# The first head's k and q projections are queued on TensorE behind the last pair's index scores of the two longest blocks

## The chip, the core and the metric

The kernel runs on one core of a Trainium2 chip. The metric is the device time of one execution in microseconds (us). The engines are TensorE (PE in the rows), VectorE (DVE), ScalarE (ACT), GpSimd (POOL) and SyncE (SP), which here only issues transfers. Each engine runs its own list of instructions in the order of the built program, so an instruction that waits holds up all that stand behind it on that engine.

## The reference, cut to what matters

One residual block over 1024 tokens of width 1024. Its mixer has two groups of heads; all their inputs come from one projection of the normed x.

```python
proj = h @ w_in
q_a, c_kv, q_idx, k_idx, w_idx, q_b, k_b, v_b, a_b, b_b, z_b = jnp.split(proj, split_points, axis=-1)
# sparse attention, per block of 128 queries
rel = jax.nn.relu(jnp.einsum('bqhd,bsd->bqhs', qi_b, k_idx))
score = jnp.einsum('bqhs,bqh->bqs', rel, wi_b)
_, idx = lax.top_k(score, topk)              # topk = 256; the chosen keys are attended to
# gated DeltaNet, 4 heads: conv and silu of q, k, v, then a recurrence over chunks of 64
t_inv = lax.linalg.triangular_solve(eye + lower, ...)
```

After the mixer come the output projection and a squared-ReLU MLP, with a norm before and behind each.

## The kernel before, in words

Products are taken in three matmuls with operands split into a high and a low part (`mm3`, L192, the matmuls are L199 to L201). A projection of 128 columns is 2 halves x 8 slices x 3 = 48 matmuls of 512 columns into one of two PSUM buffers called `two` (`project_slowly`, L333).

The stage in question, up to about 430 us, runs these generators, of which `Flow.run` (L114) picks the next by a model of time and their rank; a scheduler then sets the final order on each engine.

- `projections` (L952) goes through the plan kw, qi0 to qi3, then kb and qb of heads 0 to 3, vb0 to vb3, z0 to z3, c, qa0 to qa3. kw and qi feed the index scores; the 20 behind qi3 and kb0 (qb0 to qa3) and kb0 itself feed the rest. After kb, qb and vb a `conv` follows: one pass on ACT (L587), three on DVE (L589), a SiLU on ACT (L592). After each qb, `delta_head` (L675) makes transposes (L684), norms (L688) and Gram products (L705, L706) of that head.
- `scoring` (L460): for each pair of index heads p = 0 to 3, each block b = 7 down to 2 and each piece of its keys (320 to 512 columns) and each of the two heads, two matmuls (L471, L472) into a bank `tr` or `ch` (two of each), a ReLU on ACT in place (L478), and a multiply and add into `score` on DVE (L479). That is 80 pieces.
- `bisect` (L494) waits for "scored", the end of all scores. It finds the 256th largest score of every row bit by bit: 32 steps, each with three passes on ACT (L521) and three on DVE (L528), and a small update (L531 to L533; of the first step L536 to L538), which the next step needs. Then come the ties and the mask for six blocks (L549 to L578), on DVE.
- `base_blocks` (L711), after head 3: 31 dependent pairs of DVE operations (L725, L726) invert the diagonal blocks, a copy (L727) ends them, SP stores the result (L728) and loads it back (`diagonals`, L740).
- `levels` (L765) and `chain` (L857), which need that: POOL builds `ui` and `te` (L783), then matmuls L797, L806, L810, L822, L830, L838 alternate with small copies on ACT and DVE (L798, L807, L812, L823, L831, L839), and L870 is the first product of the recurrence.
- `post_c` (L421) ends with two DVE passes over `c_row` (L436, L437). The next stage begins with the transposes of `c_row` on TensorE (L1098) and, on SP, with loads of queries (L1057) and of w_uk and w_uv (L1089), which ACT splits (L1092) for the keys' products. L1288 loads a gain into the place of `c_row` once the transposes have read it; it is used much later.

In the kernel before, nothing but rank and the model of time sets kb0, qb0 and the following projections against the scores.

Of the kernel before, what the change touches and what calls it, by code (L numbers as in the profile page):

```python
# [18 lines left out]
P = 128  # L19
# [120 lines left out]
def block_kernel(ctx: ExitStack, tc: tile.TileContext, x, w_in, c_norm, w_uk, w_uv, rel_bias, conv_w, a_log,  # L140
# [4 lines left out]
    V, S, G, PE, SY = nc.vector, nc.scalar, nc.gpsimd, nc.tensor, nc.sync  # L145
# [18 lines left out]
    const, _ = pl.open("const")  # L164
    ps_t, _ = pl.open("ps_t", bufs=2, space=PSUM)
    ps_c, _ = pl.open("ps_c", bufs=2, space=PSUM)
    ps_w, ps_w_close = pl.open("ps_w", bufs=2, space=PSUM)
    dram, _ = pl.open("dram", space=DRAM)
# [106 lines left out]
    loaded = {}  # L275
# [12 lines left out]
    ps = psw()  # L288
# [15 lines left out]
    ps = pst()  # L304
# [3 lines left out]
    for half in range(2):  # L308
# [9 lines left out]
        for k in range(NK):  # L318
            ps = pst()
# [13 lines left out]
    def project_slowly(wts, evac, ths=(0, 1), two=False):  # L333
        wh, wl, n = wts
        both = psw() if two else None
        for th in ths:
            sl = slice(th * 512, th * 512 + 512)
            ps = both[:, sl] if two else psa()
            for k in range(NK):
                mm3(ps[:n, :], wh[:, k, :n], wl[:, k, :n], hTH[:, k, sl], hTL[:, k, sl], k == 0, k == NK - 1, True)  # L340
                yield
            evac(ps, th, sl)
        if two:
            loaded["both"] = both
# [26 lines left out]
    QS = pl.t(pi, [P, 8, T], F32R, "QS")  # L371
    KH = pl.t(pi, [P, T], F32R, "KH")
    KL = pl.t(pi, [P, T], F32R, "KL")
# [65 lines left out]
    def bias():  # L439
# [17 lines left out]
        src = bass.AP(tensor=tv_d.tensor, offset=tv_d.offset, ap=[[384, 8], [0, P], [1, 384]])  # L457
        SY.dma_start(tz_d, src)

    def scoring():  # L460

        for p in range(4):
            yield ("qi", p)
            for b in range(NB - 1, 1, -1):
                for s0, w in cuts(P * (b + 1)):
                    dst = score[:, soff[b] + s0:soff[b] + s0 + w]
                    for h in (2 * p, 2 * p + 1):
                        while flow.bank("px", 4) > flow.now:
                            yield flow.bank("px", 4)
                        ps = psx()  # L470
                        PE.matmul(ps[:, :w], QS[:, h, b * P:(b + 1) * P], KH[:, s0:s0 + w], start=True, stop=False)  # L471
                        PE.matmul(ps[:, :w], QS[:, h, b * P:(b + 1) * P], KL[:, s0:s0 + w], start=False, stop=True)  # L472
                        wh = wab[:, b, h:h + 1]
                        t = flow.pe(2 * w / 2260)
                        if h == 0:
                            V.tensor_scalar(dst, ps[:, :w], 0.0, wh, op0=OP.max, op1=OP.mult)
                        else:
                            S.activation(ps[:, :w], ps[:, :w], AF.Relu)  # L478
                            V.scalar_tensor_tensor(dst, ps[:, :w], wh, dst, op0=OP.mult, op1=OP.add)  # L479
                            t = act(t, w / 1200 + 0.18)  # L480
                        flow.took("px", dve(t, w / 960 + 0.16))
                        yield 0.0
        for b in range(NB - 1, 1, -1):
            G.memset(score[0:64, soff[b] + P * b + 64:soff[b] + P * (b + 1)], PAD)
        flow.done("scored", flow.rings["px"][-1])
# [256 lines left out]
    flow = Flow()  # L742
# [209 lines left out]
    def projections():  # L952
        nonlocal dna, dn, dn_close
        for i, (kind, p) in enumerate(plan):
            for j in range(1, 3):
                fetch(i + j)
            evac = None
            if kind == "kw":
                evac = evac_kw
            elif kind == "qi":  # L960
                evac = evac_pair(QS, p, 0.125)
            elif kind in ("kb", "qb", "vb"):
                def evac(*_):
                    pass
            elif kind == "z":
                evac = evac_spill(z_d[:, :, p, :].rearrange("n p t -> p n t"), AF.Silu, 1.0, tmp4())
            elif kind == "c":
                evac = evac_c
            else:
                evac = evac_spill(qa_d[:, p, :].rearrange("p (n t) -> p n t", t=P), AF.Copy, 0.125, tmp4())  # L970
            for _ in project_slowly(loaded[i], evac, two=True):
                flow.pe(0.64)
                yield 0.0
            if kind == "kw":
                post_kw()
                gates()
                bias()
            elif kind == "qi":
                flow.done(("qi", p), dve(act(flow.now, 1.2), 1.4))
            elif kind in ("kb", "qb", "vb"):  # L980
                blk = {"qb": 0, "kb": 4, "vb": 8}[kind] + p
                if kind == "vb":
                    conv(loaded["both"], blk, v_d[:, :, p, :])
                    act(dve(act(flow.now, 1.05), 3.7), 1.1)
                else:
                    act(dve(act(flow.now, 1.05), 3.7), 1.1)
                    if p == 0:
                        for n in range(4 * (kind == "qb"), 4 + 4 * (kind == "qb"), 2):
                            decays(n)
                    if kind == "qb" and p == 0:  # L990
                        yield "scored"
                        pi_close()
                        dna, dna_close = pl.open("dna", side="right")
                    if kind == "kb":
                        kqh = pl.t(dna if p % 2 else kq, [P, NB, 2, P], F32, "kqh")
                    a = 0 if kind == "kb" else 1
                    conv(loaded["both"], blk, q_d[:, :, p, :] if a else None, kqh[:, :, a, :])
                    if kind == "qb":
                        delta_head(p, kqh)
                        dve(act(flow.pe(5.2), 4.0), 9.5)  # L1000
                    if (kind, p) == ("qb", 3):
                        base_blocks()
                        dna_close()
                        kq_close()
                        dn, dn_close = pl.open("dn", side="right")
                        st["dt"] = pl.t(dn, [P, 2, 32, 32], F32, "dt")
                        diagonals()
                        flow.done("base", dve(flow.now + 3.0, 30.0) + 8.0)
            elif kind == "c":
                post_c()  # L1010
        yield "topk"
        flow.done("projections", flow.now)
# [16 lines left out]
    ps_a, _ = pl.open("ps_a", bufs=2, space=PSUM)  # L1029
    ps_s, _ = pl.open("ps_s", bufs=2, space=PSUM)  # L1030
# [377 lines left out]
    hlp, _ = pl.open("hl", bufs=12)  # L1408
# [45 lines left out]
    rawp, _ = pl.open("raw", bufs=2, side="right")  # L1454
    tmpp, _ = pl.open("tmp2", bufs=17, side="right")
# [119 lines left out]
    while ready:  # L1575
# [4 lines left out]
        ps = bank_[{2: 1, 3: 5, 4: 7}.get(j, j)]  # L1580
# [138 lines left out]
    while ready:  # L1719
# [8 lines left out]
        for t in range(4):  # L1728
            ps = bank_[set_][t]
# [9 lines left out]
    fin, _ = pl.open("fin")  # L1739
    rows = []  # L1740
    for f in range(NS):
# [5 lines left out]
        w = []  # L1747
# [21 lines left out]
    for tb in range(NB):  # L1769
        yt = [acc[n][:, tb % 4] for n in (("11", "12"), ("21", "22"))[tb // 4]]  # L1770
        for c in range(2):
            ps = psc() if c else pss()
# [33 lines left out]
```

## Time and profile before

| | |
|---|---|
| median of 3 runs | 1387.98 us (1382.74 to 5743.25) |
| the profiled execution | 1387.9 us |
| its span | 1386.2 us, mean granted TensorE clock 0.965 |
| TensorE / VectorE busy over the span | 93% / 80% |
| first and last score matmul (L471, L472) | 67.8 and 192.3 us |
| first step of the bisection done | 203.3 us |
| transposes of `c_row` (L1098), which open the next stage | 430.63 us |

Times in rows are counted from the span's start. A busy share over the whole span averages over stages with different limits; what the change touches lies between 70 and 440 us and is read from the rows of that stretch. PEclk is the granted clock of TensorE as a share of 2.4 GHz.

### The profile page before, as it was taken

To read this page: it belongs to the slowest core of one execution; us is meant where nothing else is said; L and a number is where in the kernel's file an instruction comes from. 1 tells how busy PE (TensorE), PEld (TensorE's weight loads), DVE (VectorE), ACT (ScalarE), POOL (GpSimd) and SP (SyncE) were. 2 spreads that over 40 slices of the span, in tenths; PEclk is the share of its full clock that TensorE was granted. 3 is DMA by queue.
4 is the path that set the end of the run, shared out by engine and by line. 5 is a ranking of instruction groups with operands and counts; after the bars stand their busy time and mean duration, and the time that the engine had idled before them with its cause. 6 is when DMAs were issued, how large, how long until landed. Compare 5 with 4: busy or idle time off the path is not lost.

```text
span 1386.2 us, 20222 instructions
## 1 busy us (share of the span) xinstructions
PE 1284.0 (93%) x6628; PEld 1110.4 (80%) x6628; DVE 1108.2 (80%) x2552; ACT 735.4 (53%) x1543; POOL 253.7 (18%) x276
## 2 busy tenths in 40 slices
PE   7899999888777999998989899999999899999995
PEld 4578888777666999877878788888887788888885
DVE  5555779999998888987677467888777987888886
ACT  5455457676624777776455456566666333333422
POOL 3112322122233444348020000000000000000023
PEclk8999999999987999999999899999999999999998
DMA  6223224445055332324355916655566975746215
GB/s 195 66 88 106 61 77 122 137 140 134 23 142 155 97 114 81 93 86 162 125 180 185 298 67 213 213 204 196 208 213 239 392 259 203 251 120 206 77 52 176
DMA packets 184146, 213.33 MB, mean 154 GB/s; under 512 B 28161, under 2 KB 123626, under 8 KB 183914
## 3 DMA queue, kind: packets, MB, share of 16 engines
q1 hardware_dynamic: 184042, 212.06, 47.2%
q8 instruction: 52, 0.85, 0.2%
q14 instruction: 52, 0.43, 0.1%
HBM read 138.58 MB, written 75.00 MB: 154 GB/s over the span
## 4 chain that ended last, share of the span: by engine, by line
PE 65%; DVE 19%; DMA 7%; ACT 5%; issue 2%; POOL 0%; SPq 0%; DVEq 0%; ACTq 0%
PE sc L199 4%; PE sc L200 4%; PE sc L201 4%; PE ch L201 4%; PE ch L199 4%; PE ch L200 4%; PE acc L199 4%; PE acc L200 4%; PE acc L201 4%; DVE pre L528 3%; PE two L199 3%; PE two L200 3%; PE two L201 3%; PE tr L199 2%; PE tr L201 2%
## 5 line engine op out<-in xcount | busy, mean ns | idle before, releaser
L199 PE MATMUL two<-hTH,wh 128*128 128x512 f32 (+1 forms) x416 | 164.5, 398 | 23.0 <-ACT tmp L409 10.6
L200 PE MATMUL two<-hTL,wh 128*128 128x512 f32 (+1 forms) x416 | 163.9, 394 | 0.0
L201 PE MATMUL two<-hTH,wl 128*128 128x512 f32 (+1 forms) x416 | 162.0, 391 | 0.0
L1763 POOL TENSOR_TENSOR tmp<-acc,c_row 128x512 f32<-128x512 f32 x16 | 20.7, 1301 | 644.1 <-DVE acc L1776 632.5
L521 ACT ACTIVATE jk<-score,cand 128x1024 bf16<-128x1024 f32 (+2 forms) x96 | 92.4, 964 | 46.8 <-DVE cand L533 36.2
L199 PEld LDWEIGHTS two<-hTH,wh 128*128 128x128 f32 (+1 forms) x416 | 80.6, 194 | 38.9 <-issue 19.7
L200 PEld LDWEIGHTS two<-hTL,wh 128*128 128x128 f32 (+1 forms) x416 | 80.8, 194 | 11.7 <-issue 0.5
L201 PEld LDWEIGHTS two<-hTH,wl 128*128 128x128 f32 (+1 forms) x416 | 80.1, 193 | 12.0 <-issue 0.5
L1426 ACT CAST hl<-raw 128x512 fp32r<-128x512 f32 x81 | 48.6, 614 | 71.4 <-PE acc L200 51.5
L269 POOL TENSOR_TENSOR wl<-stg,wh 128x1024 fp32r<-128x1024 f32 (+1 forms) x26 | 61.1, 2351 | 80.7 <-ACT wh L266 79.3
L1426 ACT CAST hl<-tt 128x512 fp32r<-128x512 f32 x56 | 34.4, 616 | 72.9 <-PE tr L200 44.6
L1426 ACT CAST hl<-tmp 128x512 fp32r<-128x512 f32 x60 | 35.8, 617 | 55.9 <-DVE tmp L1543 30.6
L1427 DVE TENSOR_TENSOR hl<-raw,hl 128x512 fp32r<-128x512 f32 x81 | 55.2, 684 | 4.5 <-ACT hl L1426 3.3
L1187 ACT CAST part<-tr 128x512 fp32r<-128x512 f32 x80 | 42.7, 542 | 27.3 <-PE tr L1185 24.0
L1162 ACT ACTIVATE big<-big,nm 128x256 f32<-128x256 f32 (+6 forms) x64 | 50.4, 789 | 11.3 <-DVE nm L1161 9.4
L1188 DVE TENSOR_TENSOR part<-tr,part 128x512 fp32r<-128x512 f32 x80 | 50.0, 629 | 4.3 <-ACT part L1187 4.0
L1210 PE MATMUL acc<-part,VS 128*128 128x256 f32 x288 | 51.7, 303 | 0.7 <-DVE part L1188 0.7
L268 POOL TENSOR_SCALAR wh<-stg 128x1024 fp32r<-128x1024 f32 x19 | 19.9, 1049 | 174.8 <-PE two L200 160.6
L589 DVE SCALAR_TENSOR_TENSOR tmp<-two,svT,tmp 128x1023 f32<-128x1023 f32 (+2 forms) x36 | 45.9, 1276 | 6.1 <-ACT tmp L587 6.0
L1138 POOL TENSOR_TENSOR mt<-tz,maskb 128x256 f32<-128x256 f32 x56 | 37.6, 681 | 59.3 <-DVE mx L1154 46.2
L199 PE MATMUL acc<-h2H,hl 128*128 128x512 f32 x120 | 46.3, 387 | 1.6 <-ACT tmp L1477 1.6
L1185 PE MATMUL tr<-ident,big 128*128 128x128 f32 x288 | 46.7, 277 | 0.5 <-DVE part L1188 0.4
(507 smaller groups left out, 4121.7 us busy)
## 6 DMA issues: line engine op xcount, KB each, us to landing
hid<-tmp SPq DMA_DIRECT2D x140, 256.0 KB, 2.6
hq<-hid SPq DMA_DIRECT2D x80, 256.0 KB, 5.3
raw<-in_w_mlp_in_dram SPq DMA_DIRECT2D x14, 1024.0 KB, 5.5
tmp<-hid SPq DMA_DIRECT2D x56, 256.0 KB, 5.4
raw<-in_w_mlp_out_dram SPq DMA_DIRECT2D x13, 1024.0 KB, 7.4
stg<-in_w_in_dram SPq DMA_DIRECT2D x25, 512.0 KB, 4.3
x<-in_x_dram SPq DMA_DIRECT2D x8, 512.0 KB, 5.3
la_d<-la SPq DMA_DIRECT2D x8, 512.0 KB
```

Source lines behind the costliest of these rows:

```text
L199: PE.matmul(o, lh, rh, start=start, stop=False, skip_group_check=more)
L200: PE.matmul(o, lh, rl, start=False, stop=False, skip_group_check=more)
L201: PE.matmul(o, ll, rh, start=False, stop=stop, skip_group_check=more)
L269: G.tensor_sub(wl[:, :, :n], f[:, :, :n], wh[:, :, :n].bitcast(F32))
L521: S.activation(junk[:, :n], s_of(b), AF.Sign, bias=cand[:, 3 + i:4 + i].bitcast(F32), scale=-1.0, accum_out=cnt[:, 3 + i:4 + i])
L589: V.scalar_tensor_tensor(acc[:, 3 - j:T], both[:, 0:T - 3 + j], w[j], acc[:, 3 - j:T], op0=OP.mult, op1=OP.add)
L1162: S.activation(pr[:, :n], pr[:, :n], AF.Exp, bias=nm, accum_out=den[:, hh:hh + 1])
L1185: PE.transpose(ps[:, c * P:(c + 1) * P], u["p"][hh][:, (j + a) * P:(j + a + 1) * P], ident)
L1188: V.tensor_sub(pt[:, 0:2 * nj, 1, :], v4(ps)[:, 0:2 * nj], pt[:, 0:2 * nj, 0, :].bitcast(F32))
L1210: PE.matmul(po[:, hh * 256:hh * 256 + 256], VS[:, j + a, 2 * p + hh, :], pt[:, 2 * a + hh].rearrange("p a t -> p (a t)"), start=j + a + hh ...
L1426: S.copy(h_, src)
L1427: eng.tensor_sub(l_, src, h_.bitcast(F32))
```

## The change

`scoring` keeps its last matmul in `behind` and raises a flag "most scored" once blocks 7 and 6 of the last pair are in the program. `projections` waits for that flag ahead of kb0 and ahead of qb0, and puts their first matmul behind the matmul then kept. No instruction is added or taken away.

```diff
+    behind = [None]
...
-                        PE.matmul(ps[:, :w], QS[:, h, b * P:(b + 1) * P], KL[:, s0:s0 + w], start=False, stop=True)
+                        behind[0] = PE.matmul(ps[:, :w], QS[:, h, b * P:(b + 1) * P], KL[:, s0:s0 + w], start=False,
+                                              stop=True)
...
+                if (p, b) == (3, 6):
+                    flow.done("most scored")
...
-            for _ in project_slowly(loaded[i], evac, two=True):
+            work = project_slowly(loaded[i], evac, two=True)
+            if kind in ("kb", "qb") and p == 0:
+
+                yield "most scored"
+                with tc.issue_after(behind[0].ins):
+                    next(work)
+            for _ in work:
                 flow.pe(0.64)
                 yield 0.0
```

The order on three engines changes as follows. On TensorE, before, from the last score piece ahead of kb0 (`two_1100` is kb0's PSUM buffer, `tr` and `ch` are score banks):

```order
L471 MATMUL ch_805<-KH_374,QS_373 128x512
L472 MATMUL ch_805<-KL_375,QS_373 128x512
L471 MATMUL tr_826<-KH_374,QS_373 128x448
L472 MATMUL tr_826<-KL_375,QS_373 128x448
L199 MATMUL two_1100<-hTH_107,wh_768 128x512
L200 MATMUL two_1100<-hTL_108,wh_768 128x512
L201 MATMUL two_1100<-hTH_107,wl_769 128x512
```

TensorE now, at kb0 (`two_1140`; a line number of this kernel is 2 to 11 higher than that of the same line before):

```order
L473 MATMUL tr_1147<-KH_374,QS_373 128x384
L474 MATMUL tr_1147<-KL_375,QS_373 128x384
L473 MATMUL ch_1125<-KH_374,QS_373 128x448
L474 MATMUL ch_1125<-KL_375,QS_373 128x448
L473 MATMUL ch_1135<-KH_374,QS_373 128x448
L474 MATMUL ch_1135<-KL_375,QS_373 128x448
L199 MATMUL two_1140<-hTH_107,wh_768 128x512
L200 MATMUL two_1140<-hTL_108,wh_768 128x512
L201 MATMUL two_1140<-hTH_107,wl_769 128x512
```

Up to `tr_826` both programs are the same on TensorE. Where kb0 began, qi3's last 24 matmuls with 6 pieces and then 37 pieces by themselves (12 of 512 columns, 8 of 448, 10 of 384, 7 of 320) now stand, then kb0's 48 matmuls with 8 pieces among them, then the last 3 pieces, and only then qb0. Before, kb0, qb0, kb1, qb1, kb2 and most of qb2 stood among the same pieces.

On VectorE, before, the end of the inversion (L725 to L727 on `kqh`) against the bisection's last step (L528 to L533):

```order
L528 TENSOR_SCALAR pre_3536,cnt_1257<-score_369,cand_1255 128x896
L531 TENSOR_SCALAR bare_1256<-cand_1255 128x6
L725 TENSOR_TENSOR kqh_2198<-kqh_2193 128x31
L528 TENSOR_SCALAR pre_3538,cnt_1257<-score_369,cand_1255 128x512
L726 TENSOR_TENSOR kqh_2193<-kqh_2193,kqh_2198 128x31
L528 TENSOR_SCALAR pre_3540,cnt_1257<-score_369,cand_1255 128x384
L727 COPY kqh_2193<-kqh_2193 128x1024
L532 TENSOR_TENSOR t_207_1259<-cnt_1257,lim_1258 128x6
L533 SCALAR_TENSOR_TENSOR cand_1255<-t_207_1259,bare_1256 128x6
```

VectorE now, at the end of the inversion (L730, L731, the copy L732) and behind it (L579 to L583 are the last two blocks' masks, L812 was L807, the first operation of `levels`):

```order
L730 TENSOR_TENSOR kqh_2213<-kqh_2208 128x31
L575 TENSOR_SCALAR jk_3622<-score_369,thr_377 128x512
L582 SCALAR_TENSOR_TENSOR jk_3609<-score_369,thr_377,jk_3609 128x640
L731 TENSOR_TENSOR kqh_2208<-kqh_2208,kqh_2213 128x31
L576 SCALAR_TENSOR_TENSOR pre_3623<-jk_3622 128x512
L583 TENSOR_SCALAR maskb_352<-jk_3609 128x640
L732 COPY kqh_2208<-kqh_2208 128x1024
```

VectorE now, ten rows behind that copy, from the last block's mask to the first operations of `levels`:

```order
L581 SCALAR_TENSOR_TENSOR jk_3635<-pre_3636,need_3639,jk_3635 128x384
L582 SCALAR_TENSOR_TENSOR jk_3635<-score_369,thr_377,jk_3635 128x384
L583 TENSOR_SCALAR maskb_352<-jk_3635 128x384
L812 TENSOR_SCALAR te_2737<-ch_2880 32x4x32
L817 TENSOR_SCALAR ui_2735<-ch_2880 32x4x32 x2
L836 TENSOR_TENSOR vk_2736<-ch_2921,sm_nk_1494 128x512
```

The inversion ended two rows ahead of the last bisection step; now it ends after the masks of the first four blocks, and 12 rows of mask stand between its copy and the first operation of `levels`. On VectorE before, six convs stood ahead of the first step's update (L538), now one, kb0's.

On SP, before, at the opening of the next stage:

```order
L762 DMA qa_3676<-la_d_358 128x4x128
L762 DMA lo_3679<-la_d_358 128x4x128
L1057 DMA q_3709<-qa_d_353 64x256 x4
L1089 DMA big_3716<-in_w_uk_dram 128x8x64
L1089 DMA big_3716<-in_w_uv_dram 128x8x64
```

SP now, at the same place:

```order
L411 DMA qa_d_353<-tmp_3237 128x1024
L1299 DMA c_row_351<-in_post_norm_mix_dram 128x1024
L767 DMA qa_3676<-la_d_358 128x4x128
L767 DMA lo_3679<-la_d_358 128x4x128
L1068 DMA q_3709<-qa_d_353 64x256 x4
L1100 DMA big_3716<-in_w_uk_dram 128x8x64
L1100 DMA big_3716<-in_w_uv_dram 128x8x64
```

The load of the gain into `c_row` (L1288 before, L1299 now) stood behind these loads and the next stage's first ones; now it stands ahead of them. Up to the transposes of `c_row` each compute engine has the same instructions in both programs, in another order.

## Rows read from the trace of the kernel before

**Rows 1.** Busy us by stretch: span:end length, PE PEld DVE ACT POOL, PEclk, DMA, GB/s.
```profile
105.00:203.00 98.00, 97.84 (x474) 86.42 (x474) 64.59 (x92) 51.45 (x101) 28.84 (x25) 1.00 0.29 83
203.00:431.00 228.00, 189.19 (x868) 161.15 (x868) 219.82 (x555) 134.12 (x275) 59.90 (x38) 0.91 0.41 115
385.00:431.00 46.00, 27.94 (x140) 23.69 (x139) 44.24 (x70) 10.84 (x28) 17.63 (x12) 0.74 0.47 114
455.00:490.00 35.00, 35.00 (x310) 33.79 (x311) 29.60 (x131) 24.93 (x71) 16.06 (x19) 1.00 0.34 101
```

**Rows 2.** Line L472: duration ns min/median/max, first and last start.
```profile
L472 PE MATMUL ch<-KL,QS x40: 302/362/522, 68.1 to 192.3; 128*128 128x512 f32 x12, 128*128 128x384 f32 x12, 128*128 128x448 f32 x8, 128*128 128x320 f32 x8
```

**Rows 3.** Timeline of DVE at the first bisection step's end: start, length, instruction.
```profile
196.83 2.60 DVE L589 SCALAR_TENSOR_TENSOR tmp<-two,svT,tmp 128x1023 f32<-128x1023 f32 x2 [1.60 <-ACT tmp L587]
...
202.33 0.68 DVE L688 TENSOR_REDUCE nr<-e 128x4 f32<-128x512 f32 x1
...
203.13 0.17 DVE L538 TENSOR_SCALAR cand<-t 128x6 int32<-128x6 int32 x1
```

**Rows 4.** Waits of DVE from 200 to 440 us: total us, times, longest.
```profile
DVE t L532 <- ACT jk L521: 3.3, 6, 1.3
```

**Rows 5.** Timeline of DVE where scores came back to back.
```profile
105.72 0.68 DVE L479 SCALAR_TENSOR_TENSOR score<-tr,wab,score 128x448 f32<-128x448 f32 x1
106.33 0.74 DVE L479 SCALAR_TENSOR_TENSOR score<-ch,wab,score 128x512 f32<-128x512 f32 x1
...
107.82 0.75 DVE L479 SCALAR_TENSOR_TENSOR score<-ch,wab,score 128x512 f32<-128x512 f32 x1
108.49 0.68 DVE L479 SCALAR_TENSOR_TENSOR score<-tr,wab,score 128x448 f32<-128x448 f32 x1
```

**Rows 6.** Timeline of PE, projection matmuls at both clock levels, and the last common score.
```profile
88.44 0.63 PE L201 MATMUL two<-hTH,wl 128*128 128x512 f32 x1
88.86 0.63 PE L199 MATMUL two<-hTH,wh 128*128 128x512 f32 x1
...
105.33 0.37 PE L472 MATMUL tr<-KL,QS 128*128 128x448 f32 x1
...
131.51 0.38 PE L200 MATMUL two<-hTL,wh 128*128 128x512 f32 x1
131.73 0.38 PE L201 MATMUL two<-hTH,wl 128*128 128x512 f32 x1
```

**Rows 7.** Busy us by stretch, as Rows 1, around scores that ran alone.
```profile
84.00:92.00 8.00, 7.10 (x24) 5.27 (x25) 6.21 (x11) 6.24 (x19) 2.07 (x2) 0.79 0.60 178
```

**Rows 8.** Timeline from the end of the inversion to the next stage, by engine.
```profile
378.79 1.07 DVE L727 COPY kqh<-kqh 128x1024 f32<-128x1024 f32 x1
...
390.41 4.71 POOL L783 TENSOR_TENSOR ui<-dt,bd 128x512 f32<-128x512 f32 x3 [12.13 <-DMA dt<-tu_d]
...
397.11 1.10 PE L797 MATMUL ch<-te,lo 128*128 128x64 f32 x8 [1.51 <-POOL te L783]
...
417.47 0.33 DVE L578 TENSOR_SCALAR maskb<-jk 128x640 bf16<-128x640 bf16 x1
...
419.76 1.11 PE L838 MATMUL ch<-ui,y 64*64 64x64 f32 x8
...
429.35 1.23 DVE L437 TENSOR_TENSOR c_row<-c_row,cn_b 128x1024 f32<-128x1024 f32 x1
...
430.63 1.76 PE L1098 MATMUL tr<-ident,c_row 128*128 128x128 f32 x7 [7.17 <-DVE c_row L437]
```

**Rows 9.** Timeline of SP, ACT and PE at the opening of the next stage.
```profile
429.91 0.59 SPq L1089 DMA_DIRECT2D big<-in_w_uk_dram  x1
...
433.64 0.62 ACT L1092 CAST UK<-big 128x512 fp32r<-128x512 f32 x1
...
437.04 0.48 PE L199 MATMUL sc<-CT,UK 128*128 128x512 f32 x1
...
440.74 0.38 SPq L1288 DMA_DIRECT2D c_row<-in_post_norm_mix_dram  x1
```

## The prediction

> **What bounds the kernel now.** I read the busy table by stretch first, then the single lines of the stage from 70 to 440 us, then its end row by row. From 105 to 203 us TensorE is the full engine: 97.84 of 98 us at full clock, while VectorE does 64.59 and idles 33.4 [rows 1]. The scores are spread through that stretch because projections stand among them; their last matmul starts at 192.3 [rows 2], and the first bisection step ends at 203.3, behind parts of a conv and of the norms (L688) of head 0 [rows 3]. From then on the roles are swapped. From 203 to 431 VectorE does 219.82 of 228 us; TensorE falls to 189.19, and at the end of the stretch to 27.94 of 46 [rows 1]. VectorE hardly waits for anybody: its largest entry from 200 to 440 us is 3.3 us in all [rows 4]. So the end of this stage is the end of VectorE's work, and the transposes of `c_row` start 0.05 us after its last pass, having waited 7.17 us for it [rows 8]. The next stage is TensorE's again (35.00 of 35 from 455 [rows 1]), so I carry a shift of its opening to the end one for one.
>
> **The change, step by step.** Nothing is removed or added, so only the place of work moves.
>
> *Scores end earlier.* Both programs are the same up to the score that starts at 105.33 [rows 6]. A projection matmul at full clock starts 0.22 us after the one before [rows 6] and a score of w columns takes the same per column, so the 24 matmuls and 6 pieces that follow need 5.2 + 2.0 us: 112.7. Then 37 pieces run alone. From below VectorE sets their pace: 0.61 us for a piece of 448 and some 0.67 for one of 512 back to back [rows 5], so in proportion 0.54 and 0.47 for the others; 12 x 0.67 + 8 x 0.61 + 10 x 0.54 + 7 x 0.47 = 21.6, and two query evacuations at 0.7 make 23: 135.7. From above, TensorE may fall to 1.2 GHz there. Where scores last ran nearly alone the granted clock was 0.79 [rows 7], and matmuls of 512 columns just behind start 0.42 apart [rows 6]; at that pace the pieces (15,808 columns, twice) cost 26, and with the evacuations 28: 141. I take 137, nearer to VectorE, since 0.79 is a mean over a stretch in which both levels show. kb0 follows: 48 x 0.22 = 10.5 and 11 pieces, 4: 151. Behind the last score there are a ReLU, an update of the score and the rest of the first step, about 5 us when no conv and no norm stands among them: first step done at 157 (154 to 162), against 203.3. That is 46 us earlier.
>
> *VectorE's debt.* Five of the six convs and the four norm reductions of head 0 now come behind that point: 15 x 1.25 [rows 3] + 4 x 0.68 [rows 3] = 21.5 us. VectorE's work between 203 and 431 is 219.8, with 8.2 idle [rows 1]. What now stands behind the inversion's copy is what before ran from the mask of the 640-column block (ends 417.8) to the end of L437 (430.6) [rows 8]: 12.8. So the copy ends at 157 + 219.8 + 21.5 - 12.8 = 385.5 plus VectorE's idle time. Before, that idle was 8 in this stretch; new are two early waits. kb0's and qb0's successors leave TensorE 10.5 us apart, while the steps between two convs need less, so the convs of qb0 and kb1 can each wait 3. I take 11 in all (5 to 20): 396.
>
> *What is late next.* Before, the copy of the inversion ended at 379.85, and its result had 50 us of bisection and masks beside it. `levels` could start at 397.11, 17.3 us later (store, load back, POOL), and was through with L838 at 420.9, still ahead of `c_row` [rows 8]. That cover is gone: 12 rows of mask, some 8 us, remain beside the 17.3. Behind L797 TensorE now has 21 projection matmuls, L806, 21, L810 and L822, 6, L830, 21, L838, and VectorE's last `c_row` pass stands behind an operation that needs L838. So: 17.3, then 21 matmuls (4.6 at full clock, 9 at half, I take 6), L806 1, 48 matmuls (10.5 to 20.6, I take 13, since the stretch before had a granted clock of 0.74 [rows 1]), five more groups of level matmuls at some 1 us each [rows 8] 5, and VectorE 1.7: 44 (40 to 55). The transposes start at 440 instead of 430.6: +9.4.
>
> *The queue of transfers.* On SP the load of the gain now stands ahead of qa, lo, the queries and w_uk, w_uv, and it overwrites `c_row`, so it waits for the transposes. Before, w_uk was issued at 429.91, ahead of the transposes, and split at 433.64, and the keys' products started at 437.04, 6.4 us behind the transposes [rows 9]. Now w_uk is issued about 2 us (transposes) and 3.7 us (gain, qa, lo, queries) behind them, needs the same 3.7 to the split: 9.4, and the products start near 10.9: +4.5. Bounds: 0, if TensorE has enough else, and 8.
>
> **Sum.** The profiled execution took 1387.9 us, the median of the runs is 1387.98, so they agree. 1387.9 + 9.4 + 4.5 = 1401.8, that is 1402, 1.0% slower. A change of under 2%, 28 us, is about what a measurement of this kernel can't tell from none.
>
> A rule that speaks against the change: the Trainium skill, "TensorE: Matmul & The Clock Gate", section "A second HAM failure mode: psum-queue depth-cycling", says that a kernel whose matmuls micro-idle between groups because they cycle through PSUM banks swings between half and full clock. This is the stretch of 37 pieces on four banks, and the granted 0.79 agrees with it. By the rule alone it would end at 141 rather than 137, and the sum would be 1406.
>
> **The rivals.**
> *The early start wins.* The 46 us less the debt of 21.5 are 24.5 us in hand. If the scores run at VectorE's pace (first step done at 154), VectorE idles only 5 and TensorE is at full clock at the end, the copy ends at 387 and the transposes start at 427; with the load of the gain hidden the kernel takes 1384. If `levels` did not wait at all, the stage would end with VectorE's work, at 157 + 219.8 + 21.5 + 11 = 409: 1367. For it speaks that VectorE bounds the stage [rows 4]; against it the place of the copy in the order. It decides from a copy that ends by 386 us.
> *TensorE takes over.* 20 projections at 10.5 follow 151, so TensorE needs until 361 for them alone, and before, 38.8 of its 228 us beside the bisection were idle [rows 1]. If convs wait for it, VectorE's idle grows to 25 and the last matmuls run at half clock: the copy ends at 410, the transposes come at 465, plus 4.5: 1427. Before, no such wait shows [rows 4], but five projections were ahead then. It decides from 22 us of VectorE idle time.
> *Absorbed.* The opening is late, but TensorE then finds more of its operands ready, and the loss is made up before 600: 1388. Against it speaks TensorE's 35.00 of 35 [rows 1].
> That the change does nothing is excluded by the order.
>
> **How the numbers follow.** Forecast (1392 to 1412) 0.5; early start 0.2 (1367 to 1384); absorbed 0.15; TensorE takes over 0.15 (1416 to 1430). The range 1374 to 1424 leaves out the ends of the second and fourth. Faster by over 2% (below 1360) needs more than the best case: 0.03. Slower by over 2% (above 1416) is the fourth: 0.15. The rest, 0.82, is within 2%.
>
> **What would show it.** Last score matmul near 151 and L538 near 157; PEclk below 1 between 113 and 137; VectorE full from 165 to 395; the copy (L732) near 396 and L797 17 us behind it; VectorE idle for over 15 us ahead of L812; SP's load of the gain ahead of w_uk, with ACT's split waiting for it. I am wrong if the copy ends by 386, if VectorE waits for convs for over 20 us, or if the next stage's length differs from before by more than 8 us.

## The result, and the profile after

The changed kernel takes 1397.9 us (median of four runs, 1395.9 to 1403.4), the kernel before 1388.8: a ratio of 1.0077, with a 95% interval of 1.0048 to 1.0106, so 10.7 us more (6.7 to 14.7). One of the four runs of the kernel before took 5743 us, and the ratio leaves it out. The prediction was 1402, within 2% and slower than before. The profiled execution is the longest of the four: 1403.4 us, a span of 1401.5 against 1386.2, 15.3 more. Of these, 3.6 stand ahead of the first score (71.7 against 68.1), where both programs are the same; the change's own share in this execution is 11.7. ("First score" is here and below the start of the second matmul of the first piece.)

Busy time by stretch in the changed kernel (length; PE, PEld, DVE, ACT, POOL busy with their instructions; PEclk; DMA share; GB/s):

```profile
105.00:203.00 98.00, 91.82 (x398) 71.58 (x397) 80.52 (x166) 69.79 (x142) 24.27 (x22) 0.97 0.25 70
117.80:142.30 24.50, 22.91 (x86) 12.98 (x85) 23.23 (x41) 20.37 (x42) 3.57 (x3) 1.00 0.22 65
163.90:400.10 236.20, 202.59 (x916) 173.02 (x915) 228.30 (x543) 141.58 (x277) 56.19 (x34) 0.94 0.36 101
400.10:438.20 38.10, 37.54 (x208) 32.33 (x207) 11.05 (x31) 6.54 (x18) 13.29 (x11) 1.00 0.65 159
```

TensorE was full from 105 to 203 before [rows 1]; now it does 91.82 of 98, and VectorE rises from 64.59 to 80.52. The second line is the stretch of scores without projections: VectorE sets the pace there, 23.23 of 24.5. From the first bisection step to the end of the inversion's copy VectorE is full, as it was from 203 to 431 before. The fourth line is new: for 38 us VectorE does 11 and TensorE 37.5. The roles are swapped at the end of the stage.

The line of the score matmuls, and the landmarks from the first bisection step to the keys' products (timeline: start, length, instruction):

```profile
L474 PE MATMUL ch<-KL,QS x40: 306/364/575, 71.7 to 156.3; 128*128 128x512 f32 x12, 128*128 128x384 f32 x12, 128*128 128x448 f32 x8, 128*128 128x320 f32 x8
```

```profile
163.92 0.17 DVE L543 TENSOR_SCALAR cand<-t 128x6 int32<-128x6 int32 x1
...
399.02 1.08 DVE L732 COPY kqh<-kqh 128x1024 f32<-128x1024 f32 x1
...
416.28 1.00 PE L802 MATMUL ch<-te,lo 128*128 128x64 f32 x8
...
437.04 0.38 PE L201 MATMUL two<-hTH,wl 128*128 128x512 f32 x1
...
438.08 0.32 SPq L411 DMA_DIRECT2D qa_d<-tmp  x1
438.22 0.86 PEld L1109 LDWEIGHTS tr<-ident,c_row 128*128 128x128 f32 x8
...
439.34 0.33 SPq L1299 DMA_DIRECT2D c_row<-in_post_norm_mix_dram  x1
...
440.77 2.47 SPq L1068 DMA_DIRECT2D q<-qa_d  x4
...
443.29 0.59 SPq L1100 DMA_DIRECT2D big<-in_w_uk_dram  x1
...
450.04 0.60 ACT L1103 CAST UK<-big 128x512 fp32r<-128x512 f32 x1
...
450.80 0.48 PE L199 MATMUL sc<-CT,UK 128*128 128x512 f32 x1
```

Line by line against [rows 2, 3, 8, 9]: the last score is 36 us earlier than before, the first bisection step 39.2; the inversion's copy is 20.2 later, the transposes 7.6, the split of w_uk 16.4 and the first product 13.8. The row at 437.04 is one that I hadn't looked at in the kernel before: TensorE's last projection matmul of the stage. Before, it started at 411.55:

```profile
411.55 0.38 PE L201 MATMUL two<-hTH,wl 128*128 128x512 f32 x1
```

In the changed kernel its evacuation and the store of that (438.08) come behind it. On SP's queue this store stands ahead of the gain, of two operands (L767), of the queries (440.77) and of w_uk, and SP stands at it from 431.3 (SP's waits from 431 to 444: total us, times, longest):

```profile
SPq L411 <- ACT tmp L409: 6.8, 1, 6.8
```

The waits of the changed kernel from 358 to 440 us (who waited for whom: total us, times, longest):

```profile
ACT jk L572 <- DVE maskb L583: 22.3, 4, 9.7
DVE te L812 <- PE ch L811: 17.7, 1, 17.7
...
PE two L199 <- ACT tmp L404: 9.2, 1, 9.2
```

The second row is the forecast one: VectorE waits for the levels' matmul that follows the late copy. The other two were not forecast. ScalarE's sign pass of a mask (L572) waits for one of two buffers that VectorE frees mask by mask; an evacuation (L404) stands behind it on ScalarE; TensorE waits for this evacuation. They aren't new, though. The kernel before has a like wait of ScalarE (its waits from 330 to 431):

```profile
ACT jk L567 <- DVE maskb L578: 11.5, 1, 11.5
```

There too evacuations came late for TensorE; the figures are below, where the two kernels' TensorE is compared.

### The profile page after: what moved, and what is told of

The parts are those of the page before. It is cut to its first block, busy times and chain, and to the rows that moved or that the text cites. A ratio compares the mean times of both kernels' runs of the same rounds, so it can differ in the third digit from the quotient of the medians.

```text
span 1401.5 us, 20229 instructions
## 1 busy us (share of the span) xinstructions
PE 1293.6 (92%) x6628; PEld 1109.6 (79%) x6628; DVE 1107.0 (79%) x2552; ACT 734.3 (52%) x1543; POOL 248.9 (18%) x276
## 5 line engine op out<-in xcount | busy, mean ns | idle before, releaser
L200 PEld LDWEIGHTS two<-hTL,wh 128*128 128x128 f32 (+1 forms) x416 | 81.3, 195 | 11.9 <-issue 0.7
L1437 ACT CAST hl<-raw 128x512 fp32r<-128x512 f32 x81 | 48.5, 614 | 70.6 <-PE acc L200 51.4
L268 POOL TENSOR_SCALAR wh<-stg 128x1024 fp32r<-128x1024 f32 x19 | 20.2, 1063 | 192.5 <-PE two L200 181.0
```

Source lines behind the costliest of these rows:

```text
L200: PE.matmul(o, lh, rl, start=False, stop=False, skip_group_check=more)
L1437: S.copy(h_, src)
```

## The experiments

All eleven variants beside the two kernels, from one profiled execution each (start times in us; the ratio is that of the timed runs to the kernel before on the same chip; e4, like e2, has the gain behind w_uv):

| kernel | ratio | first score | first step | copy | last projection | transposes | w_uk issued | products | last logits | span |
|---|---|---|---|---|---|---|---|---|---|---|
| before | 1 | 68.1 | 203.1 | 378.8 | 411.6 | 430.6 | 429.9 | 437.0 | 661.1 | 1386.2 |
| changed | 1.0077 | 71.7 | 163.9 | 399.0 | 437.0 | 438.2 | 443.3 | 450.8 | 677.6 | 1401.5 |
| e1 masks wait | 1.0087 | 71.9 | 164.1 | 378.0 | 445.2 | 439.3 | 450.7 | 458.6 | 684.4 | 1400.7 |
| e2 gain late | 1.0026 | 70.5 | 162.3 | 397.3 | 435.3 | 436.5 | 440.8 | 448.0 | 673.9 | 1392.5 |
| e3 both | 1.0084 | 71.7 | 163.9 | 377.8 | 444.9 | 439.1 | 450.4 | 458.3 | 683.1 | 1402.0 |
| e4 q only | 1.0029 | 70.2 | 165.6 | 394.1 | 431.6 | 438.7 | 437.2 | 445.8 | 670.8 | 1396.7 |
| e5 e3, ScalarE free | 1.0047 | 70.6 | 162.8 | 376.7 | 442.4 | 436.6 | 447.9 | 455.0 | 674.9 | 1394.4 |
| e6 e2, ScalarE free | 1.0038 | 71.7 | 163.9 | 402.4 | 442.5 | 443.7 | 448.0 | 454.6 | 674.5 | 1389.9 |
| e7 before, ScalarE free | 0.9973 | 69.8 | 204.9 | 380.6 | 406.8 | 432.2 | 430.6 | 438.7 | 660.3 | 1381.2 |
| e8 e6, inversion first | 0.9948 | 68.8 | 160.5 | 348.7 | 430.0 | 424.1 | 435.5 | 442.0 | 660.6 | 1376.4 |
| e9 before, e8's edits | 0.9978 | 68.3 | 203.3 | 360.1 | 404.4 | 423.9 | 436.0 | 443.3 | 665.4 | 1382.7 |
| e10 e8, ScalarE not free | 0.9993 | 68.7 | 160.3 | 348.4 | 432.3 | 426.4 | 437.8 | 444.7 | 670.8 | 1387.3 |
| e11 e8, nine steps | 0.9952 | 70.5 | 162.8 | 350.3 | 430.6 | 424.7 | 436.8 | 446.5 | 662.7 | 1385.9 |

**e1: the masks behind the inversion.** The prediction's main step says that the copy, late behind four masks, lost its cover. So the masks' first VectorE operation is queued behind the copy (not shown: a flag also keeps the masks' generator back until the inversion has been built):

```diff
-        V.tensor_copy(lb, ti.rearrange("p a b -> p b a"))
+        behind[2] = V.tensor_copy(lb, ti.rearrange("p a b -> p b a"))
...
-            V.tensor_scalar(eq[:, :n], sb, th, None, op0=OP.is_equal)
+            with tc.issue_after(behind[2].ins):
+                V.tensor_scalar(eq[:, :n], sb, th, None, op0=OP.is_equal)
```

> The change, with the masks' first VectorE operations queued behind the inversion's copy, so that its result gets the masks as cover again. Theory (the lost cover of the inversion delays the transposes of c_row by some 7.6 us): bisection ends near 358 as in the changed kernel, the copy comes near 376 instead of 399.0, levels' first product near 395 instead of 416.1, the masks end near 405, the transposes start between 415 and 428 instead of 438.2; time 1377 to 1390. Rival 1 (VectorE's debt of five convs and four norms is the loss, whatever the order): the transposes stay within 2 us of 438, time 1396 to 1400. Rival 2 (TensorE: more projections behind the scores, the last one ends at 416 in the changed kernel): levels' first product stays behind 410 and the transposes at 433 to 438; time 1393 to 1398.

Measured: 1401.8 us, ratio 1.0087 (1.0057 to 1.0118), no better than the change. The edit did what it should up to the levels: the copy is at 378.0, where it was before, and levels' first product at 401.3, 6 us behind the theory's place. Yet the transposes stay at 439.3. The theory falls. That is the place of rival 1, but not by its reason: VectorE was through with its masks at 418, and TensorE was full from there to the transposes (21.0 of 21.0 us, VectorE 6.3). What is left is TensorE, but not as rival 2 put it (the first levels' product came at 401, and the last projection of the changed kernel ends at 437, not 416); e1's busy time by stretch, its waits from 358 to 440, and ScalarE's timeline show where it stood still:

```profile
380.00:400.00 20.00, 13.38 (x53) 11.09 (x52) 19.75 (x15) 4.38 (x15) 16.52 (x9) 0.83 0.94 193
400.00:420.00 20.00, 12.40 (x53) 10.58 (x52) 18.22 (x28) 3.51 (x10) 5.97 (x4) 0.79 0.13 53
```

```profile
ACT jk L573 <- DVE maskb L585: 15.4, 2, 9.9
ACT jk L573 <- DVE need L581: 11.5, 2, 9.1
...
PE two L199 <- ACT tmp L409: 9.4, 3, 6.6
...
PE ch L813 <- ACT y L805: 7.6, 1, 7.6
```

```profile
391.69 0.94 ACT L573 ACTIVATE jk<-score,thr 128x768 bf16<-128x768 f32 x1 [9.87 <-DVE maskb L585]
...
392.62 0.58 ACT L409 ACTIVATE tmp<-two 128x512 f32<-128x512 f32 x1
```

TensorE does 25.8 of these 40 us. The evacuation L409 came right behind a sign pass that had waited 9.87 us for a mask, and the levels' copy L805, for which L813 waits, came at 414.1 behind the last of them. By moving the masks back, the edit moved ScalarE's waits with them, and the last projection went from 437.0 to 445.2.

**e2: the load of the gain behind w_uv.** The last step of the prediction alone, undone (`behind[1]` is the load of w_uv):

```diff
-        SY.dma_start(gain, bcast(post_norm_mix, P))
+        with tc.issue_after(behind[1].ins):
+            SY.dma_start(gain, bcast(post_norm_mix, P))
```

> The change, with only the load of the gain queued on SP behind w_uv again. Theory (the gain ahead of w_uk costs some 4.5 us, at most 8): transposes unchanged at 438, w_uk issued ahead of or with them instead of 5.1 us behind, the keys' products 6 to 8 us behind the transposes instead of 12.6; time 1390 to 1394. Rival (the products wait for something else, so the gain's place costs nothing): products still 11 to 13 us behind the transposes; time 1396 to 1400.

Measured: 1392.7 us, ratio 1.0026 (1.0007 to 1.0045): the time is the theory's, 5.2 below the change by the medians. But the place isn't. SP and TensorE at the opening of the next stage in e2:

```profile
435.28 0.38 PE L201 MATMUL two<-hTH,wl 128*128 128x512 f32 x1
...
436.45 1.09 PE L1109 MATMUL tr<-ident,c_row 128*128 128x128 f32 x8
```

```profile
438.17 2.58 SPq L1068 DMA_DIRECT2D q<-qa_d  x4
440.79 0.59 SPq L1100 DMA_DIRECT2D big<-in_w_uk_dram  x1
```

w_uk is still 4.3 us behind the transposes, the products 11.5 (448.0 - 436.5) instead of 12.6. So the gain's place costs about 1 us there, not 4.5. What holds w_uk is the store of the last projection ahead of it in SP's queue: it is issued at 436.31, and the seven issues from there to w_uk take 4.5 us without a wait. The rest of the 5 us comes much later: from the last logits to the end of the span e2 takes 718.6 us, the changed kernel 723.9. Whether that part is shorter by this build, or by the execution (the changed kernel's profile is its longest run), was not settled.

**e3: both edits.**

> The change with both edits: masks behind the inversion's copy, and the gain behind w_uv. Theory (two separate costs that add): the sum of the two gains, transposes between 415 and 428 and products 6 to 8 us behind them; time 1370 to 1384, so under the kernel before. Rival 1 (VectorE's debt): 1390 to 1394, only the gain's part. Rival 2 (TensorE): 1387 to 1392.

Measured: 1400.7 us, ratio 1.0084 (1.0056 to 1.0111). The gains don't add, because e1's was none: last projection at 444.9, products 13.4 us behind it.

**e4: only the q projection waits.**

```diff
-            if kind in ("kb", "qb") and p == 0:
+            if kind == "qb" and p == 0:
```

> Only the q projection of head 0 waits for the scores; the k projection stays where it was before, ahead of the last pair's evacuations, so one conv more is done early. In the built order the first bisection step comes as early as in the changed kernel, the inversion's copy stands behind three masks instead of four, and the gain is behind w_uv. Theory: first bisection step near 164, copy near 390, transposes near 430, products 6 to 8 us behind; time 1385 to 1391, as the kernel before. Rival (the early scores as such cost, by TensorE or by VectorE waiting): copy behind 396, time 1394 to 1402.

Measured: 1393.8 us, ratio 1.0029 (1.0007 to 1.0051), at the rival's lower end. First step at 165.6 as expected, with one conv less behind it; the copy at 394.1 and the products 7.1 us behind the transposes lie near the theory, the transposes at 438.7 don't. With the last projection at 431.6 w_uk is issued 1.5 us ahead of the transposes. The cost lies between before and the change, and so does the last projection (431.6).

**e5 and e6: ScalarE freed.** The sign pass needs only its sum; its unused output goes into the mask's own place instead of a shared buffer, and each of the six masks has its own counter:

```diff
-            j1 = pl.t(ph, [P, T], BF16, "jk", bufs=2)
-            sg = pl.t(ph, [P, 1], F32, "sg", bufs=2)
-            S.activation(j1[:, :n], sb, AF.Sign, bias=th, scale=-1.0, accum_out=sg)
+            sg = pl.t(ph, [P, 1], F32, "sg", bufs=6)
+            S.activation(maskb[:, moff[b]:moff[b] + n], sb, AF.Sign, bias=th, scale=-1.0, accum_out=sg)
```

e5 is e3 with this edit:

> The kernel of e3 (masks behind the inversion's copy, gain behind w_uv), and ScalarE's six sign passes of the masks write their unused output into the mask's own place and six counters, so that they no longer wait for a buffer that VectorE frees mask by mask, and the evacuations of the last projections no longer stand behind such a wait. Theory (in e3 TensorE took over: it idled 14 us from 380 to 420 because its evacuations waited on ScalarE behind the sign passes, and its last projections ended behind the transposes): ScalarE's waits for masks vanish, TensorE is busy for over 17 of 20 us from 380 to 400, the transposes come between 422 and 431 instead of 439.1, w_uk is issued before 436; time 1380 to 1390, so 10 to 20 us below e3 and not above the kernel before. Rival (TensorE has simply too much left, or the order of its queue decides, and ScalarE's waits lie beside it): transposes at 436 to 440, time 1396 to 1402.

Measured: 1393.4 us, ratio 1.0047 (1.0032 to 1.0061). Better than e3, but short of the theory, and the transposes (436.6) are in the rival's place. TensorE from 380 to 400 is full, as the theory said; then it stands still again. Busy time of e5, its VectorE and its TensorE behind that hole:

```profile
380.00:400.00 20.00, 19.74 (x98) 17.09 (x97) 19.72 (x16) 4.05 (x14) 15.58 (x9) 1.00 0.85 191
```

```profile
407.50:417.60 10.10, 0.00 (x0) 0.00 (x0) 9.74 (x22) 0.00 (x0) 0.00 (x0) 0.64 0.00 0
```

```profile
416.98 0.26 DVE L584 TENSOR_SCALAR maskb<-jk 128x384 bf16<-128x384 bf16 x1
417.27 0.28 DVE L813 TENSOR_SCALAR te<-ch 32x128 f32<-32x128 f32 x1
```

```profile
417.61 1.06 PE L816 MATMUL ch<-ui,y 128*32 128x32 f32 x16 [10.19 <-DVE te L813]
```

L816 needs L813's result, L813 stands behind all six masks on VectorE, and the remaining projections stand behind L816 on TensorE. In the changed kernel VectorE waited at this operation (L812 there) for the levels' matmul ahead of it; now TensorE waits for it with the one behind it.

e6 is e2 with ScalarE freed:

> The kernel of e2 (the change with the gain behind w_uv), with the sign passes freed as in e5, but the inversion still behind four masks. Theory (here the inversion's copy at 397 is what ends last, so TensorE's 9 us wait for ScalarE at 382 costs nothing): copy and levels' first product unchanged at 397 and 414, transposes at 434 to 437; time 1390 to 1393, as e2. Rival (ScalarE's wait is the whole loss, by itself): transposes at 428 or earlier, time 1382 to 1387.

Measured: 1392.9 us, ratio 1.0038 (1.0025 to 1.0051): the time as expected, as e2. The places are worse than expected: without ScalarE's pauses VectorE does more of the masks ahead of the copy (402.4), and TensorE waits 9.9 us for levels' operand; the transposes come at 443.7.

**e7: the kernel before with ScalarE freed.**

> The kernel before, with the sign passes freed as in e5. Theory (before, the stage ends with VectorE's last pass over c_row, whatever ScalarE waits for): transposes at 429 to 431, time 1386 to 1391, as before. Rival (ScalarE's wait of 11.5 us costs there too): transposes at 425 or earlier, time 1378 to 1385.

Measured: 1383.8 us, ratio 0.9973 (0.9957 to 0.9990). Both are wrong in part: the time is the rival's, but the transposes come at 432.2, 1.6 late like the first score (1.7), so the end of the stage didn't change, although the last projection comes 4.8 earlier (406.8). Of the 5.0 us in the span 4.2 come behind the last logits (720.9 against 725.1) and the rest ahead of them. What shortens that part is open; one profile of each kernel can't tell it from the spread between executions.

**e8: the inversion first.** Instead of the masks, the last seven bisection steps are queued behind the copy, so that the inversion runs in one piece and levels beside the bisection:

```diff
+            if bit == 6:
+                yield "inverse"
...
-                V.tensor_scalar(junk[:, :n], sb, cand[:, i:i + 1].bitcast(F32), ...
+                with tc.issue_after(behind[2].ins) if bit == 6 else ExitStack():
+                    V.tensor_scalar(junk[:, :n], sb, cand[:, i:i + 1].bitcast(F32), ...
```

with e2's and e6's edits kept (the flag "inverse" is raised once the inversion has been built).

> The kernel of e6 (the change, gain behind w_uv, ScalarE's sign passes freed), with the bisection's last seven steps on VectorE queued behind the inversion's copy, so that the inversion runs in one piece from some 324 us and levels runs beside the bisection; the last pass over c_row then stands among the masks, not behind levels' wait. Theory (the earlier scores are a real gain of VectorE time, and the order of inversion, masks and levels in two in-order queues ate it): copy near 346, levels' first product near 363, VectorE full until its last mask near 415 with no idle entry over 5 us, transposes at 412 to 424 and products close behind; time 1368 to 1383, so 10 to 25 us below e6 and below the kernel before. Rival (TensorE: five more projections behind the scores keep it until 435 whatever VectorE does): transposes at 432 or later or TensorE full from 360 to 440; time 1388 to 1396.

Measured: 1381.3 us, ratio 0.9948 (0.9929 to 0.9967), 11.6 below e6 by the medians, and the lowest median of all thirteen kernels. Landmarks of e8:

```profile
348.73 1.07 DVE L734 COPY kqh<-kqh 128x1024 f32<-128x1024 f32 x1
```

```profile
370.96 1.00 PE L804 MATMUL ch<-te,lo 128*128 128x64 f32 x8
...
424.10 1.04 PE L1112 MATMUL tr<-ident,c_row 128*128 128x128 f32 x8
...
430.02 0.38 PE L201 MATMUL two<-hTH,wl 128*128 128x512 f32 x1
...
441.95 0.74 PE L199 MATMUL sc<-CT,UK 128*128 128x512 f32 x1
```

The time is within the theory's range, near its upper end, and the order is as meant: VectorE works through to its last mask at 424.9, no wait of levels shows on it, the transposes come at 424.1. The places are later than the theory's, levels' first product by 8 us and the last mask by 10. And the products are 17.9 us behind the transposes and 11.9 behind the last projection: the transposes are not what the next stage waits for any more.

**e9: e8's edits in the kernel before** (there the last eight steps).

> The kernel before, with the same three edits as e8 (bisection's last eight steps behind the inversion's copy, freed sign passes, gain behind w_uv). Theory (before, VectorE's work ends the stage, so an earlier inversion alone gives nothing; e8's gain needs the earlier scores): VectorE full until its last mask, which still ends at 424 to 430, transposes not before 425; time 1380 to 1386, as the kernel before with freed sign passes (1383.8). Rival (the earlier inversion is the gain by itself): within 4 us of e8.

Measured: 1385.8 us, ratio 0.9978 (0.9964 to 0.9993), like e7 and within the theory's range; the rival (within 4 us of e8) misses by 0.5. The edits without the earlier scores bring what freeing ScalarE alone brings. The transposes come at 423.9, earlier than the theory allowed, since c_row's pass now stands among the masks; but the masks themselves last until 432.7, 8 us longer than in e8 (line of e9's masks: durations, first and last start):

```profile
L582 DVE TENSOR_SCALAR maskb<-jk x6: 260/326/408, 411.0 to 432.7; 128x1024 bf16<-128x1024 bf16 x1, 128x896 bf16<-128x896 bf16 x1, 128x768 bf16<-128x768 bf16 x1, 128x640 bf16<-128x640 bf16 x1
```

The inversion isn't in one piece here: 33 other VectorE instructions stand inside it (3 in e8), and its copy comes at 360.1, 11 us later than in e8.

**e10: e8 with ScalarE not freed.**

> e8 without the freed sign passes, which is e2 (the change, gain behind w_uv) with the last seven bisection steps behind the inversion's copy. Theory (the place of the inversion is the main part of e8's gain over e2; ScalarE's waits for masks matter less once levels runs ahead of the masks): copy near 349, transposes at 424 to 431, time 1380 to 1387, so 6 to 13 us below e2. Rival (the freed sign passes bring it, as they bring 4 us to the kernel before): time within 2 us of e2's 1392.7.

Measured: 1388.3 us, ratio 0.9993 (0.9978 to 1.0008), 1.3 above the theory's range and 2.4 below the rival's, so nearer to the theory. With e2, e6 and e8 it makes a square: freeing ScalarE alone changes e2 by nothing (1.0026 and 1.0038), putting the inversion first alone brings 4.4 us, both bring 11.4.

**e11: two more bisection steps behind the copy.**

> e8 with nine instead of seven bisection steps behind the inversion's copy. Theory (in e8 the stage no longer ends with VectorE's chain but with TensorE's last projections and the loads queued behind them, products 18 us behind the transposes): transposes earlier by 3 to 10 us, but products of the keys within 3 us of e8's 441.9; time 1378 to 1384, as e8. Rival (VectorE's order still decides): products at 436 or earlier, time 1370 to 1377.

Measured: 1382.9 us, ratio 0.9952 (0.9935 to 0.9969), as e8. The transposes don't come earlier (424.7, with a first score 1.7 later than e8's), the products at 446.5 are 2.8 later when that is taken off. The time and the products are the theory's, the transposes aren't. Nor did the edit make the inversion earlier: its first operation waits 2.2 us for the load of its input, and the copy comes at 350.3 for 348.7, the same with the late start taken off. What a still earlier inversion would be worth isn't shown.

## Why the prediction was right, and where it was right for another reason

*The scores.* 37 pieces without projections were to take 23 us at VectorE's pace; they take 22.5 (119.8 to 142.3). The 24 matmuls and 6 pieces ahead of them took 10.5 us (109.3 to 119.8) for 7.2, with TensorE at the lower clock level from 111.1 to 114.5. The last score starts at 156.3, or 152.7 with the late opening taken off, for 151. The rule of the Trainium skill ("TensorE: Matmul & The Clock Gate", "A second HAM failure mode: psum-queue depth-cycling") would have had TensorE swing to half clock there and end at 141; the granted clock of 117.8 to 142.3 is 1.00, so the measurement decides against it for this stretch, and against the prediction's own sign of a clock below 1 up to 137.

*The first step* was put 5 us behind the last score, with no conv in between, although the order on VectorE left kb0's conv there; it came 7.6 behind. The three passes of this conv (1.27 each) stand among the last updates. That is a mis-sized term: the start is 39 us earlier (42.8 with the late opening taken off), not 46.

*VectorE's debt.* From the first step to the end of the copy it was to work 219.8 + 21.5 - 12.8 = 228.5 us and idle 11; it works 228.3 and idles 7.9. The copy ends at 400.1 for 396, all of it from the late opening and the step above.

*What is late next.* The levels' first product is 16.2 us behind the copy's end, for 17.3, and the transposes 38.1, for 44. The 69 projection matmuls were priced at 19 us, between both clock levels; the granted clock was 1.00 throughout, and at 0.215 each they take 14.9. Transposes: 438.2 for 440; against before +7.6, of which 4.0 are the change's own, for +9.4.

*The queue of transfers.* The products came 12.6 us behind the transposes, for 10.9: +6.2 against before, for +4.5. Here the number was near and the cause was wrong. By e2 the gain is about 1 us of it. In the ten kernels with early scores SP issues w_uk 5.5 to 6.2 us behind TensorE's last projection (5.5 to 5.6 in eight of them; 6.2 in e11 and in the changed kernel, where the gain stands between), since the store of this projection is ahead of w_uk on SP. In the kernel before the last projection was 18.4 us ahead of w_uk and held nothing up; there, as in e9, SP's queue last waited for VectorE's masks (before, 405 to 431 us, and e9, 405 to 437):

```profile
SPq L762 <- DVE maskb L578: 7.1, 1, 7.1
```

```profile
SPq L766 <- DVE maskb L582: 23.8, 1, 23.8
```

In both w_uk is issued 3.0 us behind the end of the last mask (426.9 and 433.0). The last projection is the step that the prediction left out. It had TensorE's load as a rival that decides by VectorE's idle time (from 22 us on); VectorE idled 7.9, and TensorE still came late. No run puts w_uk ahead of that store, so what this alone would save isn't shown.

The two kernels' TensorE from the last score that they have in common (105.33 before, 109.29 here) to the end of its last projection, before and changed:

```profile
105.20:411.90 306.70, 278.40 (x1290) 240.03 (x1290) 266.46 (x606) 180.70 (x359) 84.59 (x59) 0.96 0.38 106
```

```profile
109.20:437.40 328.20, 291.64 (x1332) 242.75 (x1332) 281.09 (x645) 183.82 (x373) 81.11 (x60) 0.95 0.37 101
```

TensorE's waits in these stretches, before and changed:

```profile
PE two L199 <- ACT tmp L409: 10.6, 2, 5.9
PE two L199 <- ACT tmp L404: 7.1, 1, 7.1
PE tr L705 <- DVE la L706: 3.9, 2, 2.2
```

```profile
PE tr L710 <- DVE la L711: 9.6, 3, 4.3
PE two L199 <- ACT tmp L404: 9.2, 1, 9.2
PE two L199 <- ACT tmp L409: 8.9, 5, 2.7
PE two L199 <- DVE t L537: 4.9, 1, 4.9
```

The same scores and projections take 21.5 us longer. 8.9 of them are the lone pieces: 15,808 columns twice at 0.22 us per 512 are 13.6, and they took 22.5. Projections had filled these gaps before. The waits for ScalarE's evacuations are not a part of it: they are 18.1 us here and 17.7 before. Waits for VectorE outside the scores are a part (16.0 us here, 6.8 before), and so are small matmuls of levels that now stand ahead of the last projection.

*One for one.* "I carry a shift of its opening to the end one for one" held for the changed kernel by its build only: +13.8 at the products, +16.3 at the first logits, +16.5 at the last, +15.3 at the end. In the others it didn't: from the last logits to the end the kernels take between 715 and 726 us, and e1, 23.3 late at the last logits, is 14.5 late at the end. The reason for that spread stays open.

So the sum was right (+13.9 forecast; +11.7 in the profile without the late opening; 10.7 timed) with a first term too large by 5, a second too small by 2, and a wrong name on the second. That they come so near is in part luck. The prediction also took a change of under 28 us for about what can't be told from none; 10.7 us came out with an interval of 6.7 to 14.7.

The theory that the late copy alone is the loss fell with e1; what stands is that in-order queues hold each other. The early scores give VectorE time back (the last mask ends at 405.0 instead of 426.9), but TensorE needs 21.5 us more for its own part, and SP's queue, which was held by a mask, is now held by the store of TensorE's last projection. Freeing ScalarE and putting the inversion first together bring 11.4 us, either alone 0 and 4.4.

Whether the early start is worth anything once these are out of the way is not settled. e8 is 4.5 us faster than e9 by the medians, clear of the runs' spread, but e9's inversion is not in one piece. Against e7, the kernel before with nothing but ScalarE freed, e8 is 2.5 us faster, which the spread of the runs doesn't separate.

## What to carry to other kernels

Where one engine is full and another has room, work taken from between its instructions doesn't only move: the full engine gets gaps that this work had filled, so price the lost filling on the engine that you unload, and follow its last instruction of the stage as well as the bound engine's. Before you count a wait as the price of a change, look for it in the kernel before. In in-order queues a wait that is taken away in one place can come out on another engine (the inversion's copy, the sign pass, the levels' evacuation); removing one of several such waits may bring nothing, and two together the gain, so test them in pairs. And when a transfer is late, look at which entry ahead of it in its queue waits, and for whom, before you blame the newcomer.

## What the runs showed of the hardware

- With the same program ahead of it, the first score started between 68.1 and 71.9 us in the thirteen profiled executions. A single pair of profiles carries up to 3.8 us of this, more than a third of the effect here.
- Scores alone on four accumulation banks, with VectorE setting the pace, ran with a granted clock of 1.00 from 117.8 to 142.3, two waits of 0.80 and 0.57 us for VectorE included. A stretch at the lower level came just ahead, from 111.1 to 114.5 (0.51 granted from 111.0 to 114.5), after two waits of 0.77 us for VectorE: matmuls of 512 columns there start 0.43 apart instead of 0.22. The kernel before did the same from about 86.6 to 89.7, after two waits of 0.81 us [rows 6, 7]; a single wait of 0.76 us ahead of 105.02 was followed by no fall.
- A transfer with its operands ready still waits for its turn to be issued: in e2 SP took 4.5 us for the seven issues from the store at 436.31 to w_uk at 440.79, and none of those behind the store waited for another engine.
